# Where the seven-product couples stand in the ConvGLU of a two-layer encoder trunk, how many there are, and when the last gated tiles are raised

## The chip, the cores and the metric

The kernel runs on one core of a Trainium2 chip. A core has a matrix engine (TensorE, called PE in the profile, with PEld for its weight loads) and three elementwise engines: VectorE (DVE), ScalarE (ACT) and GpSimd (POOL). SyncE (SP) only issues DMA transfers here. Each engine takes its instructions in the order in which the program lists them, and they wait for one another by semaphores. SBUF is the on-chip memory; PSUM is where matmuls accumulate, in banks of 128 x 512 float32.

The metric is the device time of one execution in microseconds (us), lower is better. The kernel before takes 2427.54 us, the median of 3 runs (2427.39 to 2429.62).

## The reference

The input x has 256 tokens of width 2048. Two layers follow, each a pre-norm token mixer (layer 0 an mLSTM, layer 1 an HGRN2 recurrence) and a pre-norm ConvGLU. The change touches the ConvGLU alone:

```python
D_MODEL, SEQ, DEPTH, D_FF, CONV_W = 2048, 256, 2, 5504, 3

def conv_glu(hn, w_up, conv_w, conv_b, w_down):
    u = hn @ w_up                                  # (256, 2048) @ (2048, 11008)
    a, v = jnp.split(u, 2, axis=-1)
    ap = jnp.pad(a, ((0, 0), (1, 1), (0, 0)))
    c = conv_b
    for j in range(CONV_W):
        c = c + ap[:, j:j + 256] * conv_w[j]       # depthwise, along the tokens
    return (jax.nn.gelu(c, approximate=False) * v) @ w_down   # (256, 5504) @ (5504, 2048)

for layer in range(DEPTH):
    h = h + mixer(rmsnorm(h, norm_mix_g[layer]))
    h = h + conv_glu(rmsnorm(h, norm_ffn_g[layer]), ...)
out = rmsnorm(h, final_g)
```

## The kernel before

**Numbers.** All weights are float32 and are streamed once from HBM. For the matrix engine each operand is split into a high part, rounded to the reduced format fp32r, and a low part, what the rounding left. A product of two operands is three matmuls: high by high, high by low, low by high. For weights the high part `wh` is a cast on ACT (line 172 in the ConvGLU) and the low part `wl` a subtraction on DVE (line 173). There are four buffers of 1024 columns each for `wh` and for `wl`, and three of 2048 columns for the raw weights that a DMA fills; the split runs three pieces ahead of the matmuls.

**The ConvGLU.** The 43 tiles of 128 columns of D_FF are worked in three parts of 16, 16 and 11. A part first runs its up groups, of four tiles each (the last group of the part of 11 has three), and then a pair of down products, one for each half of the 2048 output columns. Groups and halves are objects of class `Pair`. A `Pair` walks its contraction in couples of two 128-row tiles: 8 couples for an up group (2048 rows) and for a down pair of a part of 16, and five couples and a half one ("H") for a down pair of the part of 11. A plan string names the form of each couple:

- "N" is the plain form. Two token halves by two column halves by two contraction tiles make 8 products, 24 matmuls of 512 columns.
- "S" is a Strassen-like form. It makes 7 products, 21 matmuls, from sums and differences of the operands. The weight differences are three DVE subtractions into the tile `T4` (lines 189, 191 and 192; of 1024, 512 and 512 columns). `T4` then goes through the same split as the raw weights: an S couple gives four pieces to split (of 1024, 512, 1024 and 1024 columns), an N couple two (of 1024). The differences of the x operand (`form`, split in its turn by lines 358 and 359) are made once per couple position and serve all `Pair`s that share x. N couples that stand before the last S of a plan need a small form too.
- Beside its four accumulators `c11` to `c22` (tiles `c1` and `c2`), a `Pair` with S couples needs three banks `m1`, `m6` and `m7`. It takes them at its first S. After its last S, `middle` adds them up into the SBUF tile `at` (`combine`, lines 1050 to 1054) and in a down pair adds `at` into the residual `hx` (line 1098). When all couples are through, `done` adds the accumulators (line 1083 in an up group, 1103 in a down pair).

**Raising.** A finished up group lies in `at` with tokens as rows. `raise_up` turns it tile by tile: four PE transposes per tile into a bank `pt` (line 1011), then ACT scale (1013), two DVE shifts of the convolution (1014 and 1015), ACT Gelu (1016), DVE product with v (1017), and the split into the gated tile `g` (1019 and 1020), plus the forms that the down plan wants. It is a side job: it makes a step whenever the matmul emitter's own clock (0.68 per product) has gone on by the value that the job yields. The banks `m1`, `m6`, `m7`, `pt` and all other small PSUM tiles come from one pool of four.

**What sets the order.** The code emits work in the order just told, and a scheduler that keeps a timeline of its own then places each engine's instructions. The order printed below is what it left. `UP_PLAN` and `DOWN_PLAN` in lines 23 and 24 are the two tables that the change edits.

Of the kernel before, what the change touches and what calls it, by code (L numbers as in the profile page):

```python
# [19 lines left out]
FT = 5504 // P  # L20
PARTS = ((0, 16), (16, 16), (32, 11))
GROUP = 4
UP_PLAN = "NNSNSNNN"
DOWN_PLAN = {16: "NNSNSNNN", 11: "NNNNNH"}
AH = 8
BH = 16
EPS = 1e-6
# [30 lines left out]
def trunk_kernel(ctx, tc, xT, x_d, fg_d, pp_d, cst_d, w_first, w_aq, w_ak, w_av, w_ao, w_aout,  # L58
# [59 lines left out]
    side = Side()  # L118
# [860 lines left out]
    def ffn(layer, norm, nxt):  # L979
# [17 lines left out]
        def raise_up(st):  # L997
            while not st["ready"]:
                yield 0.5
            at, w = st["at"], st["w"]  # L1000
            mp = box["mp"]
            for j in range(w // P):
                f, i = st["f"] + j, st["i"] + j
                if i % 2 == 0:
                    st["GT"].c2 = mp.tile([P, 2, T], F32, tag="c2", bufs=2, name="c2")
                c = st["GT"].c2[:, i % 2]
                pt = aux("pt")
                for n in range(2):
                    for t in range(2):
                        o = n * T + t * P  # L1010
                        pe.transpose(pt[:, o:o + P], at[:, t, n * 512 + j * P:n * 512 + (j + 1) * P], ident)  # L1011
                cw = [col("conv_w", (layer * 3 + k) * FT + f) for k in range(3)]
                act.activation(c, pt[:, 0:T], AF.Identity, scale=cw[1], bias=col("conv_b", layer * FT + f))
                dve.scalar_tensor_tensor(c[:, 1:T], pt[:, 0:T - 1], cw[0], c[:, 1:T], ALU.mult, ALU.add)
                dve.scalar_tensor_tensor(c[:, 0:T - 1], pt[:, 1:T], cw[2], c[:, 0:T - 1], ALU.mult, ALU.add)
                act.activation(c, c, AF.Gelu)
                dve.tensor_tensor(c, c, pt[:, T:2 * T], ALU.mult)
                g = slot(i, "g")
                act.copy(g[:, 0:T], c)
                dve.tensor_tensor(g[:, T:2 * T], c, g[:, 0:T].bitcast(F32), ALU.subtract)  # L1020
                st["GT"].x[i] = g
                if i % 2 and i // 2 in st["GT"].want:
                    st["GT"].forms[i // 2] = forms(st["GT"].c2, st["GT"].want[i // 2], mp, f"gf{i // 2}", mp)
                yield 2.5
            st["over"] = True

        class Gated:
# [29 lines left out]
        before = None  # L1057
        for part, (f0, nf) in enumerate(PARTS):
            GT = Gated(nf)
            for i in range(0, nf, GROUP):  # L1060
                w = min(GROUP, nf - i) * P
                st = dict(f=f0 + i, i=i, GT=GT, w=w, wait=[before] if before else [])
                before = st

                def middle(acc, st=st):
# [7 lines left out]
                def done(acc, st=st):  # L1073
                    w = st["w"]
                    plain = "at" not in st
                    if plain:
                        room(st)
                    for t in range(2):
                        d, v, sc = rows(acc["rows"][t], w), rows(st["at"][:, t], w), norm.rc[:, t:t + 1]
                        if plain:  # L1080
                            act.activation(v, d, AF.Copy, scale=sc)
                        else:
                            dve.scalar_tensor_tensor(v, d, sc, v, ALU.mult, ALU.add)
                    st["ready"] = True
                st["ready"] = False
                ch = Pair(w_up[layer, (f0 + i) // GROUP], UP_PLAN, norm.x, norm.form, lambda acc, done=done, st=st: (done(acc), side.push(raise_up(st))),
                          middle, w=w)
                ch.pool = lambda: box["mp"]
                chunks.append(ch)
            before = dict(wait=[before], over=True)  # L1090
# [43 lines left out]
    nf = FinalNorm()  # L1134
# [109 lines left out]
```

## Time and profile before

| what | value |
|---|---|
| median of 3 runs | 2427.54 us |
| the profiled execution | 2427.81 us, of which the span of its instructions is 2426.0 us |
| granted clock of the matrix engine, mean | 0.998 of full speed |
| ConvGLU of layer 0, first to last product of its `Pair`s | about 402 to 1115 us from the span's start |
| ConvGLU of layer 1, first product | 1704 us |

Times in the views are microseconds from the first instruction. In a row of instructions, `c<-wh,xt` reads "tile c written from tiles wh and xt", buffer numbers are left out (so `m` is any of m1, m6 and m7, and `T` is T4), `x16` is a count, and L207 is line 207 of the kernel. An engine's busy time says little when its work lies beside that of the engine that sets the pace, so the views that matter are those of one up group or one down pair.

Names for the stretches below: U0 to U3 are the four up groups of a part of 16 and D0 and D2 its two down pairs. The stretches quoted are of layer 0, part 1 (the second part), which runs from 666.8 to 929.4 us.

### The profile page before, as it was taken

What the parts mean: (1) busy time and instruction counts of PE and PEld (TensorE: products, weight loads), DVE (VectorE), ACT (ScalarE), POOL (GpSimd) and SP (SyncE); (2) the same over time, 40 slices, a digit from 0 to 9 for tenths busy, and PEclk for the clock granted to TensorE, in tenths of its full rate; (3) what the DMA queues carried; (4) which work ended last, traced back from release to release, by engine and by line L of the source; (5) the groups of instructions that cost most, each with busy time, mean ns of one, the idle gap of its engine ahead of it and who ended that gap; (6) DMA issues with size and microseconds to landing.
All of it is one profiled execution on the core that took longest, in us unless ns stands there. A gap on an engine that the chain in (4) does not pass through costs nothing.

```text
span 2426.0 us, 34357 instructions
## 1 busy us (share of the span) xinstructions
PE 2408.5 (99%) x13201; PEld 2012.4 (83%) x13201; DVE 1938.8 (80%) x2883; ACT 1364.1 (56%) x2024; POOL 165.1 (7%) x219
## 2 busy tenths in 40 slices
PE   9999999999999999999999999999999999999998
PEld 7888888888888888888888888888878888888886
DVE  7766667888889888866888889886798888987885
ACT  6655455656456555655555555555566555654654
POOL 0100000000000000001222222220000000000000
PEclk9999999999999999999999999999999999999999
DMA  7654555555655555465545544555555555556563
GB/s 288 199 182 157 191 174 174 197 185 186 207 179 199 185 195 205 163 210 170 171 172 174 173 166 168 173 174 178 187 181 201 191 196 189 175 204 208 177 208 137
DMA packets 65620, 451.73 MB, mean 186 GB/s; under 512 B 7584, under 2 KB 8096, under 8 KB 14000
## 3 DMA queue, kind: packets, MB, share of 16 engines
q1 hardware_dynamic: 63216, 442.91, 53.2%
q0 software_dynamic: 1232, 5.31, 0.9%
q8 instruction: 104, 1.70, 0.3%
q10 hardware_dynamic: 1008, 1.32, 0.2%
q14 instruction: 60, 0.49, 0.1%
HBM read 447.35 MB, written 2.16 MB: 185 GB/s over the span
## 4 chain that ended last, share of the span: by engine, by line
PE 97%; DVE 1%; ACT 1%; DMA 1%; issue 1%; SPq 0%; POOLq 0%; POOL 0%; ACTq 0%; DVEq 0%
PE c L207 49%; PE mm L330 10%; PE mm L321 7%; PE mm L320 7%; PE mm L322 7%; PE mm L337 5%; PE m L207 5%; PE pt L1011 2%; PE pn L676 1%; PE pd L863 1%; PE py L911 1%; PE pz L428 0%; PE pa L863 0%; DVE wl L173 0%; ACT wh L172 0%
## 5 line engine op out<-in xcount | busy, mean ns | idle before, releaser
L172 ACT CAST wh<-raw 128x1024 fp32r<-128x1024 f32 (+3 forms) x513 | 490.4, 987 | 323.4 <-PE c L207 303.1
L173 DVE TENSOR_TENSOR wl<-raw,wh 128x1024 fp32r<-128x1024 f32 (+3 forms) x513 | 576.0, 1144 | 115.3 <-ACT wh L172 113.8
L207 PE MATMUL c<-wh,xt 128*128 128x512 f32 (+1 forms) x2024 | 654.3, 389 | 0.9 <-ACT wh L172 0.4
L165 DVE TENSOR_TENSOR wl<-raw,wh 128x1024 fp32r<-128x1024 f32 (+1 forms) x340 | 414.2, 1222 | 196.4 <-ACT wh L164 195.6
L164 ACT CAST wh<-raw 128x1024 fp32r<-128x1024 f32 (+1 forms) x340 | 350.2, 1033 | 323.9 <-PE mm L322 163.8
L207 PEld LDWEIGHTS c<-wh,xt 128*128 128x128 f32 x2024 | 379.0, 188 | 73.1 <-ACT wh L172 3.3
L207 PE MATMUL c<-wl,xt 128*128 128x512 f32 (+1 forms) x1012 | 391.2, 388 | 0.4 <-DVE wl L173 0.4
L330 PE MATMUL mm<-xt,wh 128*128 128x512 f32 x1024 | 361.4, 396 | 0.9 <-DVE hx L1103 0.9
L207 PE MATMUL c<-wh,g 128*128 128x512 f32 x1000 | 323.7, 393 | 1.1 <-DVE hx L1103 0.9
L337 PE MATMUL mm<-xt,wl 128*128 128x256 f32 x1024 | 289.4, 283 | 0.0
L330 PEld LDWEIGHTS mm<-xt,wh 128*128 128x128 f32 x1024 | 192.1, 188 | 44.6 <-issue 1.3
L207 PE MATMUL c<-wh,F 128*128 128x512 f32 (+1 forms) x600 | 228.2, 390 | 0.0
L207 PEld LDWEIGHTS c<-wl,xt 128*128 128x128 f32 x1012 | 190.3, 188 | 40.4 <-DVE wl L173 6.2
L207 PEld LDWEIGHTS c<-wh,g 128*128 128x128 f32 x1000 | 187.7, 188 | 40.2 <-issue 2.1
L172 ACT CAST wh<-T 128x1024 fp32r<-128x1024 f32 (+1 forms) x120 | 124.7, 1039 | 141.8 <-PE c L207 139.2
L320 PE MATMUL mm<-wh,xt 128*128 128x512 f32 x512 | 202.1, 395 | 2.2 <-ACT xt L342 1.7
L321 PE MATMUL mm<-wl,xt 128*128 128x512 f32 x512 | 201.7, 394 | 0.6 <-DVE wl L165 0.6
L322 PE MATMUL mm<-wh,xt 128*128 128x512 f32 x512 | 200.7, 392 | 0.1
L207 PE MATMUL c<-wl,g 128*128 128x512 f32 x500 | 195.5, 391 | 0.0
L337 PEld LDWEIGHTS mm<-xt,wl 128*128 128x128 f32 x1024 | 193.3, 189 | 1.3
L173 DVE TENSOR_TENSOR wl<-T,wh 128x1024 fp32r<-128x1024 f32 (+1 forms) x120 | 144.8, 1207 | 59.8 <-ACT wh L172 58.5
L207 PEld LDWEIGHTS c<-wh,F 128*128 128x128 f32 x600 | 112.7, 188 | 23.5
(259 smaller groups left out, 3361.7 us busy)
## 6 DMA issues: line engine op xcount, KB each, us to landing
raw<-in_w_up SPq DMA_DIRECT2D x160, 1024.0 KB, 4.8
raw<-in_w_down SPq DMA_DIRECT2D x79, 1024.0 KB, 4.8
raw<-in_w_bq SPq DMA_DIRECT2D x48, 1024.0 KB, 5.0
raw<-in_w_ao SPq DMA_DIRECT2D x16, 1024.0 KB, 4.8
raw<-in_w_aout SPq DMA_DIRECT2D x16, 1024.0 KB, 4.8
raw<-in_w_bv SPq DMA_DIRECT2D x16, 1024.0 KB, 4.9
raw<-in_w_bg SPq DMA_DIRECT2D x16, 1024.0 KB, 4.8
raw<-in_w_bout SPq DMA_DIRECT2D x16, 1024.0 KB, 4.8
```

The source lines that it names most:

```text
L164: act.copy(wh[:, :m], r)
L165: dve.tensor_tensor(wl[:, :m], r, wh[:, :m].bitcast(F32), ALU.subtract)
L172: act.copy(wh[:, :m], r)
L173: dve.tensor_tensor(wl[:, :m], r, wh[:, :m].bitcast(F32), ALU.subtract)
L207: pe.matmul(acc[name][:, 0:w], a, b, start=name not in begun, stop=sp and i == 2)
L320: pe.matmul(ps[t], xh, wh[:, c], start=st, stop=False)
L321: pe.matmul(ps[t], xh, wl[:, c], start=False, stop=False)
L322: pe.matmul(ps[t], xl, wh[:, c], start=False, stop=sp)
L330: pe.matmul(ps[f], wh[:, c:c + P], x, start=st, stop=False)
L337: pe.matmul(ps[f][:, 0:T], wl[:, c:c + P], x[:, 0:T], start=False, stop=sp)
L676: pe.matmul(pn[:, 0:258], w, v, start=(i == 0), stop=(i == len(parts) - 1))
L1011: pe.transpose(pt[:, o:o + P], at[:, t, n * 512 + j * P:n * 512 + (j + 1) * P], ident)
```

## The change

Four tables and numbers change; no instruction of a new kind appears.

1. Up groups of a part, all but the last: `NNSNSNNN` becomes `SNSNSNNN`, three S couples in place of two.
2. The last up group of each part gets a plan of its own, `SNSNNNNN`: still two S couples, at the first and third place in place of the third and fifth.
3. Down pairs of 16: `NNSNSNNN` becomes `SNSNNNNN`, two S couples as before, at the first and third place.
4. Down pairs of 11: `NNNNNH` becomes `SNNNNH`, one S couple where there was none, and so `m1`, `m6`, `m7`, a `combine` and two additions into `hx` where there were none.
5. The raising of the last group of each part yields 0.8 in place of 2.5 after each tile, so its tiles follow each other sooner in the emitted order.

```diff
-UP_PLAN = "NNSNSNNN"
-DOWN_PLAN = {16: "NNSNSNNN", 11: "NNNNNH"}
+UP_PLAN = "SNSNSNNN"
+UP_LAST = "SNSNNNNN"
+PACE = 2.5
+PACE_LAST = 0.8
+DOWN_PLAN = {16: "SNSNNNNN", 11: "SNNNNH"}
...
-                yield 2.5
+                yield PACE_LAST if st['end'] else PACE
...
-                st = dict(f=f0 + i, i=i, GT=GT, w=w, wait=[before] if before else [])
+                st = dict(f=f0 + i, i=i, GT=GT, w=w, end=i + GROUP >= nf, wait=[before] if before else [])
...
-                ch = Pair(w_up[layer, (f0 + i) // GROUP], UP_PLAN, norm.x, norm.form, ...
+                ch = Pair(w_up[layer, (f0 + i) // GROUP], UP_LAST if i + GROUP >= nf else UP_PLAN, norm.x, norm.form, ...
```

After the change every line number that is named here is larger by 3 (207 is 210, 1083 is 1086).

Three places show how the instructions move. The first is DVE at the border between U0 and U1 (layer 0, part 1), where `done` of U0 (the two rows on `at<-c`) meets the first pieces of U1. Before, U1 begins with N couples, and T4 of its first S is made early:

```order
L173 TENSOR_TENSOR wl<-raw,wh 128x1024 x4
L189 TENSOR_TENSOR T_6040<-raw 128x1024
L1083 SCALAR_TENSOR_TENSOR at<-c_5726,rc,at 128x1024
L191 TENSOR_TENSOR T_6040<-raw,T_6040 128x512
L1083 SCALAR_TENSOR_TENSOR at<-c_5727,rc,at 128x1024
L192 TENSOR_TENSOR T_6040<-raw,T_6040 128x512
L173 TENSOR_TENSOR wl<-raw,wh 128x1024 x2
L1014 SCALAR_TENSOR_TENSOR c_6054<-pt,pp,c_6054 128x255
```

The same border on DVE after the change, from the last piece of U0 on:

```order
L176 TENSOR_TENSOR wl<-raw,wh 128x1024
L195 TENSOR_TENSOR T_6009<-raw,T_6009 128x512
L176 TENSOR_TENSOR wl<-raw,wh 128x512
L1086 SCALAR_TENSOR_TENSOR at<-c_5748,rc,at 128x1024
L1086 SCALAR_TENSOR_TENSOR at<-c_5749,rc,at 128x1024
L176 TENSOR_TENSOR wl<-T_6009,wh 128x1024 x2
L176 TENSOR_TENSOR wl<-raw,wh 128x1024 x2
L192 TENSOR_TENSOR T_6134<-raw 128x1024
L1017 SCALAR_TENSOR_TENSOR c_6075<-pt,pp,c_6075 128x255 x2
```

The two T4 pieces of U1's first S now stand behind `done` of U0 on DVE, and T4 of the second S and the first raised tiles follow at once.

The second place is DVE at the last S couple of U1 (its T4 is T_6202 before and T_6243 after), with the raising of U0's tiles between its pieces. Before:

```order
L191 TENSOR_TENSOR T_6202<-raw,T_6202 128x512
L173 TENSOR_TENSOR wl<-raw,wh 128x512
L357 TENSOR_TENSOR fe<-c_6114 128x256
L1020 TENSOR_TENSOR g_6154<-c_6114,g_6154 128x256
L173 TENSOR_TENSOR wl<-T_6202,wh 128x1024
L192 TENSOR_TENSOR T_6202<-raw,T_6202 128x512
L359 TENSOR_TENSOR F<-fe,F 128x256
L173 TENSOR_TENSOR wl<-T_6202,wh 128x1024
L173 TENSOR_TENSOR wl<-raw,wh 128x1024 x2
```

And on DVE after, at the third S couple of U1:

```order
L194 TENSOR_TENSOR T_6243<-raw,T_6243 128x512
L358 TENSOR_TENSOR fe<-c_6075,fe 128x128
L176 TENSOR_TENSOR wl<-T_6243,wh 128x1024
L1018 SCALAR_TENSOR_TENSOR c_6158<-pt,pp,c_6158 128x255
L195 TENSOR_TENSOR T_6243<-raw,T_6243 128x512
L362 TENSOR_TENSOR F<-fe,F 128x512
L1020 TENSOR_TENSOR c_6158<-c_6158,pt 128x256
L176 TENSOR_TENSOR wl<-T_6243,wh 128x1024
L176 TENSOR_TENSOR wl<-raw,wh 128x1024 x3
L1023 TENSOR_TENSOR g_6169<-c_6158,g_6169 128x256
```

Before, the fourth tile `g` is finished at this point; now only the third is, and the fourth is raised in the plain couples that follow.

The third place is PE in U1, where the products into `m6` (m_6169 before, m_6066 after; c_6032 and c_6033 before, and c_6063 and c_6064 after, are the accumulators c1 and c2) stand against the transposes. Before, at the first S couple:

```order
L207 MATMUL c_6033<-wl,F 128x512
L207 MATMUL c_6033<-wh,F 128x512
L207 MATMUL m_6170<-wl,F 128x512
L207 MATMUL m_6170<-wh,F 128x512
L207 MATMUL m_6169<-wh,F 128x512
L207 MATMUL c_6033<-wh,xt_3287 128x512
```

And on PE after, at the second S couple, where the first product into `m6` of the first S couple has been put off to:

```order
L210 MATMUL m_6066<-wh,F 128x512
L210 MATMUL m_6066<-wl,F 128x512
L210 MATMUL m_6066<-wh,F 128x512 x2
L210 MATMUL c_6064<-wl,F 128x512
L210 MATMUL c_6064<-wh,F 128x512
L210 MATMUL m_6067<-wl,F 128x512
L210 MATMUL m_6067<-wh,F 128x512
L210 MATMUL c_6064<-wh,xt_3290 128x512
L1014 MATMUL pt<-cst,at 128x128 x4
```

The bank that `m6` takes holds a `pt` until then, and with three of the four banks in use for `m1`, `m6` and `m7` the later tiles are transposed one at a time through the fourth.

More of the change, by code (lines that the diff above doesn't have):

```diff
@@ L1085, in ffn @@
                 st["ready"] = False
-                ch = Pair(w_up[layer, (f0 + i) // GROUP], UP_PLAN, norm.x, norm.form, lambda acc, done=done, st=st: (done(acc), side.push(raise_up(st))),
+                ch = Pair(w_up[layer, (f0 + i) // GROUP], UP_LAST if i + GROUP >= nf else UP_PLAN, norm.x, norm.form, lambda acc, done=done, st=st: (done(acc), side.push(raise_up(st))),
                           middle, w=w)
```

## The prediction

> **What bounds the kernel now.** I read the page first: busy times and the chain that ended last.
>
> ```profile
> span 2426.0 us, 34357 instructions
> PE 2408.5 (99%) x13201; PEld 2012.4 (83%) x13201; DVE 1938.8 (80%) x2883; ACT 1364.1 (56%) x2024; POOL 165.1 (7%) x219
> PE 97%; DVE 1%; ACT 1%; DMA 1%; issue 1%; SPq 0%; POOLq 0%; POOL 0%; ACTq 0%; DVEq 0%
> ```
>
> PE makes 97% of the chain, so a matmul taken away is time saved, unless what feeds PE is late. Whether it is late is a question of each stretch, so next comes the view by stretches, each from the first product of a `Pair` to that of the next, in layer 0, part 1: U0 to U3, D0, D2, then U1 and U2 of the part of 11 and its first down pair.
>
> ```profile
> core 0: us, PE busy (x) PEld busy (x) DVE busy (x) ACT busy (x) POOL busy (x), PEclk, DMA share, GB/s
> 666.80:709.00 42.20, 42.20 (x188) 34.95 (x187) 33.12 (x33) 22.56 (x25) 0.00 (x0) 1.00 0.58 200
> 709.00:753.40 44.40, 44.40 (x203) 36.18 (x202) 38.81 (x52) 27.54 (x39) 0.00 (x0) 1.00 0.56 189
> 753.40:798.00 44.60, 44.60 (x203) 36.28 (x202) 38.70 (x54) 27.68 (x39) 0.00 (x0) 1.00 0.55 188
> 798.00:842.90 44.90, 44.82 (x204) 36.25 (x203) 39.99 (x54) 27.40 (x38) 0.00 (x0) 1.00 0.55 189
> 842.90:887.20 44.30, 44.30 (x203) 36.25 (x202) 39.01 (x49) 24.80 (x35) 0.00 (x0) 1.00 0.56 190
> 887.20:929.40 42.20, 42.20 (x188) 34.91 (x187) 33.94 (x34) 20.61 (x23) 0.00 (x0) 1.00 0.58 201
> 971.60:1016.00 44.40, 44.40 (x204) 36.10 (x202) 37.74 (x49) 26.50 (x37) 0.00 (x0) 1.00 0.50 167
> 1016.00:1050.60 34.60, 34.40 (x203) 33.78 (x203) 29.78 (x44) 22.28 (x37) 0.00 (x0) 1.00 0.59 199
> 1050.60:1083.10 32.50, 31.61 (x146) 25.81 (x145) 22.89 (x37) 17.84 (x24) 0.00 (x0) 1.00 0.60 208
> ```
>
> U0 and D2 have 186 products and nothing else on PE: 42.2 us. Stretches with raising have 16 transposes more and take 44.3 where PE never waits (D0), so a transpose costs 2.1 / 16 = 0.13. U1 waits about 0.1, U2 0.3, U3 0.6. DVE has 5.6 us to spare in U1, but 9.1 in U0. That spare is what the change spends.
>
> How far DVE is ahead is seen in the rows themselves. DVE at the end of U1's second S couple:
>
> ```profile
> 732.85 0.70 DVE L192 TENSOR_TENSOR T<-raw,T 128x512 f32<-128x512 f32 x1
> 733.45 0.43 DVE L359 TENSOR_TENSOR F<-fe,F 128x256 fp32r<-128x256 f32 x1
> 734.72 1.23 DVE L173 TENSOR_TENSOR wl<-T,wh 128x1024 fp32r<-128x1024 f32 x1 [0.84 <-ACT wh L172]
> 735.86 2.35 DVE L173 TENSOR_TENSOR wl<-raw,wh 128x1024 fp32r<-128x1024 f32 x2
> ```
>
> and PEld just there:
>
> ```profile
> 737.13 0.19 PEld L207 LDWEIGHTS c<-wl,xt 128*128 128x128 f32 x1 [0.37 <-DVE wl L173]
> ```
>
> The first piece of the last row ends near 735.86 + 1.22 = 737.08, and the weight load that reads it starts at 737.13: the lead of DVE over PE is already used up once per group, at its last S couple. In the plain couples it comes back, up to what four buffers hold. The wait there is the T4 chain: last subtraction ended (733.55), cast on ACT, next piece at 734.72, which is 1.17 us.
>
> **The change, part by part.**
>
> *Fewer matmuls.* Every S in place of an N saves 3 matmuls. Eight up groups of each layer (3 + 3 + 2) get a third S, 16 in all; pairs of the part of 11 get one each, two in layer 0 and one in layer 1 (its other half is no `Pair`). 19 x 3 = 57, all of 512 columns, since the three-tile group keeps two S. The price of one is PE's start-to-start:
>
> ```profile
> 929.17 0.39 PE L207 MATMUL c<-wh,g 128*128 128x512 f32 x1
> 929.39 0.39 PE L207 MATMUL c<-wh,xt 128*128 128x512 f32 x1
> ```
>
> about 0.22, and over D2 42.2 / 186 = 0.2267. So 57 x 0.2267 = **12.9 us less** on PE.
>
> *More work on DVE.* The groups of U1:
>
> ```profile
> L173 DVE TENSOR_TENSOR wl<-raw,wh 128x1024 fp32r<-128x1024 f32 x14 | 16.9, 1223 | 3.0 <-ACT wh L172 3.0
> L173 DVE TENSOR_TENSOR wl<-T,wh 128x1024 fp32r<-128x1024 f32 x4 | 4.9, 1224 | 1.3 <-ACT wh L172 1.3
> L1083 DVE SCALAR_TENSOR_TENSOR at<-c,rc,at 128x1024 f32<-128x1024 f32 x2 | 2.6, 1284 | 0.3 <-PE c L207 0.2
> L189 DVE TENSOR_TENSOR T<-raw 128x1024 f32<-128x1024 f32 x2 | 2.4, 1222 | 0.0
> L191 DVE TENSOR_TENSOR T<-raw,T 128x512 f32<-128x512 f32 x3 | 2.1, 686 | 0.0
> L1014 DVE SCALAR_TENSOR_TENSOR c<-pt,pp,c 128x255 f32<-128x255 f32 x4 | 1.9, 481 | 0.9 <-ACT c L1013 0.9
> ...
> L1020 DVE TENSOR_TENSOR g<-c,g 128x256 fp32r<-128x256 f32 x4 | 1.7, 422 | 0.0
> ...
> L173 DVE TENSOR_TENSOR wl<-raw,wh 128x512 fp32r<-128x512 f32 x2 | 1.4, 693 | 0.0
> ```
>
> The next instruction starts before the one ahead has ended:
>
> ```profile
> 751.79 1.28 DVE L1083 SCALAR_TENSOR_TENSOR at<-c,rc,at 128x1024 f32<-128x1024 f32 x1
> 752.99 0.68 DVE L191 TENSOR_TENSOR T<-raw,T 128x512 f32<-128x512 f32 x1
> 753.61 1.28 DVE L1083 SCALAR_TENSOR_TENSOR at<-c,rc,at 128x1024 f32<-128x1024 f32 x1
> 754.81 0.68 DVE L192 TENSOR_TENSOR T<-raw,T 128x512 f32<-128x512 f32 x1
> 755.41 2.35 DVE L173 TENSOR_TENSOR wl<-raw,wh 128x1024 fp32r<-128x1024 f32 x2
> ```
>
> so 512 columns cost 0.60 (754.81 to 755.41) and 1024 cost 2.35 - 1.22 = 1.13. An S adds 1.13 + 2 x 0.60 of subtractions and turns two pieces of 1024 into three and one of 512, 1.13 + 0.60 more: **4.1 us of DVE per S**. The form at position 0 is now the large one, +0.7 in U1 (four operations of 128 and one of 512 for two of 256, scaled from the same rows); U2 and U3 lose forms at places 3 and 4. Hence U1: 38.8 + 4.1 + 0.7 = 43.6 of DVE against 44.4 - 0.7 = 43.7 of PE, U2 about 42.2 of 43.9. In U0 37.2 of 41.5: covered.
>
> *Whether U1 holds.* From the order, between the second `done` row of U0 and the last T4 piece of the third S, DVE has 14 instructions of 1024 columns, 7 of 512, 5 of 256, 4 of 128, 6 shifts and the `done` row: 14 x 1.13 + 7 x 0.60 + 5 x 0.33 + 4 x 0.20 + 6 x 0.40 + 1.20 = 26.1 (256 and 128 scaled by 1.13 - 0.60 per 512 columns; a shift 481 - 422 = 59 ns over a 256). PE has, from U0's last matmul to the one that reads that piece, 109 matmuls and 16 transposes: 24.7 + 2.1 = 26.8. DVE starts `done` after that last matmul:
>
> ```profile
> 753.17 0.63 PE L207 MATMUL c<-wh,xt 128*128 128x512 f32 x2
> ```
>
> against 753.61 above: 0.44 later. The T4 chain adds 1.87 (1.17 and the subtraction's 0.70) where the order gives it 0.60 + 0.60 + 0.33: 0.3. DVE is through at 0.44 + 26.1 + 0.3 + 0.1 = 26.9 against 26.8, and the piece behind is needed 4 matmuls (0.9) later for 1.13 of work: PE waits 0.3. Waits of DVE for ACT in the same place before were the 0.84 above, mostly this chain; a few tenths more are likely. Bounds: 0 (no gaps, the lead carried over from the plain couples) and 2.5 (the idle of DVE ahead of the T4 pieces, the shifts and `done` in U1 before: 1.3 + 0.9 + 0.3 in the groups above; the 3.0 ahead of the plain pieces is mostly full buffers). I take a wait of 0.6 for U1 and U2, nearest to the sum, 0.4 more than now. Ten groups have three S and raising: **+4.0**.
>
> *Last groups and 16-wide down pairs* (U3, D0, D2) keep their S count; the S couples come first, behind `done`. U3's DVE loses a form (1.4): -0.1 each, **-0.4** for four. In D0 the tiles of U3 are raised in the same stretch as the S couples; the faster pace moves them nearer, but three of the four banks are held, so they still go one at a time. The last tile must be there for the last couple, 40 us into D0, and in the order it stands about 5 us ahead. I take +0.2 for each D0 (0 to 1): **+0.8**. D2 and U0 have no raising: 0.
>
> *Pairs of 11.* DVE gets an S (4.1), a `combine` (1.13 + 2 x 0.60) and two additions of 1.13: 22.9 + 8.7 = 31.6 against 31.8 of PE, with raising ending in mid-pair. Before, this pair waited 0.9 (32.50 against 31.61 busy), and the new work lies behind the plain couples' slack: 0, bounds -0.7 and +1 each.
>
> *First group of each layer* begins with an S whose form comes straight from the norm, and holds three banks while the last x tiles are transposed: 0 to 1, I take 0.2, **+0.4** for both.
>
> *ACT and DMA.* An S adds a cast of 1024 and one of 512 to ACT, some 1.5 us on 27.5 of 44. Bytes are the same; T4 needs its raw tile whole, and waited for DMA twice in layer 0:
>
> ```profile
>   DMA raw<-in_w_up: 2.1, 2
> ```
>
> with DMA at 0.55 to 0.60 in the stretches, I take 0. SP issues the same transfers, POOL is untouched.
>
> Sum: -12.9 + 4.0 - 0.4 + 0.8 + 0.4 = -8.1. The profiled execution took 2427.8, of which 2426.0 is the span; its time stands 0.3 above the median. 2427.8 - 8.1 = 2419.7, against the median 2419.4; I say **2419.5 us**.
>
> [...] By the rows above DVE overlaps: 1.28 long, the next 1.20 later. [...]
>
> **The rivals.**
>
> *The cover holds everywhere.* DVE goes ahead in the plain tails, the ten groups wait as little as U1 and U2 now: 2427.5 - 12.9 to -14 = 2413.5 to 2415. For it: the sum is a tie. Against: the lead was already at 0.05 us in U1 with two S.
>
> *DVE gaps take most of it.* Each of the ten groups waits 1 to 1.8 instead of 0.2: -12.9 + 10 x 0.8 to 1.6 + 0.8 = -4 to +4, 2423 to 2431.
>
> *Slower: the raise chain blocks PE.* PE's fourth set of transposes in U1 waits for the one free bank, released by the product row L1020 (1017 before), and stands in PE's queue before the last `m6` products; by the sums above that release comes only 0.2 us ahead of PE's place. If DVE keeps the 2.5 us of idle that it had there, every one goes straight to PE: ten groups x 2.3 = 23, less 12.9: about +10, 2437. It decides from 1.3 us of gaps per group on. Against it: much of that idle was DVE standing at full buffers.
>
> *Slower: DVE cannot overlap.* If each DVE instruction cost its whole length, U1 would need the sum of its durations, some 43 by its groups, plus 1.22 + 2 x 0.69 + 1.22 + 0.69 = 4.5: 47.6 and so 3.2 more than now in ten groups, +32 less 9 x 0.7 elsewhere: 2453. The overlap in the rows speaks against it. [...]
>
> **How the numbers follow.** A measurement here tells 0.2% (4.9 us) from no change. My forecast, 2416 to 2422.7: 0.48. Cover holds: 0.17. Gaps take most: 0.20, nearly all of it within 0.2%. Blocked raise chain: 0.11. No overlap: 0.02; elsewhere slower: 0.02. So faster 0.65, same 0.20, slower 0.15. The range 2414 to 2429 leaves out the two slower cases and the edges of the others, about 0.2; the likeliest case alone spans 2416 to 2422.7.
>
> **What would show it.** PE matmuls 57 fewer. U0 and D2 at 41.5 and 42.2 without waits. U1 and U2 near 44.2, with PEld waiting for `wl` at the third S; DVE above 42 busy there. D0 near 44.5. The forecast is wrong if U1 takes over 45 (gaps), if PE waits before `pt` or the first `m6` (banks), or if the part of 11's pairs grow by over a microsecond.

## The result and the profile after

The changed kernel takes 2418.45 us, the median of 5 runs (2417.42 to 2418.99), against 2429.61 us (2427.39 to 2430.08) of the kernel before on the same chip: a ratio of 0.9956, 95% interval 0.9942 to 0.9971. The forecast was 2419.5 us. The profiled execution has a span of 2416.7 us, 9.3 us less than before. The sum is close, its terms are not: U3, put at -0.4 us, and D2 with the later U0, put at 0, turned out at -3.2 and +3.0.

The lines of the page that answer to those shown of before (span, busy times, engine shares of the chain):

```profile
span 2416.7 us, 34392 instructions
PE 2396.5 (99%) x13144; PEld 2001.0 (83%) x13144; DVE 2015.4 (83%) x2993; ACT 1393.4 (58%) x2062; POOL 166.0 (7%) x219
PE 90%; DVE 7%; issue 1%; ACT 1%; DMA 1%; SPq 0%; POOLq 0%; POOL 0%; ACTq 0%; DVEq 0%
```

There are 57 matmuls fewer (13201 to 13144), and DVE now stands in 7% of the chain instead of 1%: PE waits more often for what DVE makes. The same nine stretches as in the prediction (U0 to U3, D0, D2 of layer 0, part 1, then U1, U2 and the first down pair of the part of 11):

```profile
core 0: us, PE busy (x) PEld busy (x) DVE busy (x) ACT busy (x) POOL busy (x), PEclk, DMA share, GB/s
665.60:707.40 41.80, 41.80 (x184) 34.15 (x183) 35.58 (x36) 23.87 (x27) 0.00 (x0) 1.00 0.58 201
707.40:751.70 44.30, 44.21 (x201) 35.68 (x201) 43.41 (x59) 29.02 (x41) 0.00 (x0) 1.00 0.52 173
751.70:796.10 44.40, 44.12 (x201) 35.65 (x200) 42.68 (x57) 28.85 (x40) 0.00 (x0) 1.00 0.56 193
796.10:840.10 44.00, 44.00 (x203) 36.45 (x202) 37.45 (x47) 27.27 (x37) 0.00 (x0) 1.00 0.56 194
840.10:884.20 44.10, 44.10 (x204) 36.46 (x203) 39.56 (x49) 25.04 (x35) 0.00 (x0) 1.00 0.53 185
884.20:926.80 42.60, 42.60 (x187) 34.70 (x186) 33.90 (x33) 20.60 (x23) 0.00 (x0) 1.00 0.62 216
968.60:1012.80 44.20, 44.11 (x200) 35.64 (x199) 41.74 (x57) 28.11 (x40) 0.00 (x0) 1.00 0.51 170
1012.80:1047.40 34.60, 34.60 (x203) 33.75 (x202) 31.27 (x47) 22.79 (x37) 0.00 (x0) 1.00 0.57 188
1047.40:1078.10 30.70, 30.70 (x143) 25.39 (x142) 28.22 (x36) 18.14 (x25) 0.00 (x0) 1.00 0.55 186
```

U1 and U2 lost three matmuls each, 0.68 us, but only 0.2 us of their length. U3, which lost none, is 0.8 us shorter; D2 is 0.4 us longer; the pair of 11 is 1.8 us shorter. Where PE now stands, read from the weight loads (PEld) of part 1, in U0, U1 and D2 (the bracket holds the wait before the row and what ended it):

```profile
668.27 0.19 PEld L210 LDWEIGHTS c<-wh,xt 128*128 128x128 f32 x1 [0.21 <-ACT wh L175]
691.17 0.19 PEld L210 LDWEIGHTS c<-wl,xt 128*128 128x128 f32 x1 [0.33 <-DVE wl L176]
...
732.92 0.42 PEld L1014 LDWEIGHTS pt<-cst,at 128*128 128x128 f32 x4 [0.49 <-PE m L210]
734.01 0.19 PEld L210 LDWEIGHTS c<-wh,xt 128*128 128x128 f32 x1 [0.40 <-ACT wh L175]
735.46 0.19 PEld L210 LDWEIGHTS c<-wl,xt 128*128 128x128 f32 x1 [0.38 <-DVE wl L176]
...
886.93 0.19 PEld L210 LDWEIGHTS c<-wh,g 128*128 128x128 f32 x1 [0.29 <-ACT wh L175]
899.67 0.19 PEld L210 LDWEIGHTS c<-wl,g 128*128 128x128 f32 x1 [0.33 <-DVE wl L176]
```

U1's waits for weights are at its third S couple, as forecast, and make 0.40 + 0.38. Just ahead of them the transposes of the fourth raised tile wait too (the row at 732.92). That row names PE's own product, but DVE's product L1020, the last reader of the one free bank, ended within 0.1 us of it:

```profile
732.39 0.41 DVE L1020 TENSOR_TENSOR c<-c,pt 128x256 f32<-128x256 f32 x1
```

In all ten raising groups with three S these transposes start 0.15 us after L1020 has ended, and 0.25 to 0.52 us behind PE's pace, 3.8 us in all. So PE does wait before `pt`, which the prediction named as a sign of the bank rival. It costs little by itself, because the weights wanted next come later still: in run 2 below U1 of part 1 has no such wait and is only 0.14 us shorter.

But U0 and D2, where nothing is raised and DVE has 6 and 9 us to spare, wait as well: at the opening couple and at the last one, 0.21 + 0.33 and 0.29 + 0.33. An S couple takes 1.13 + 2 x 0.60 of differences and 3 x 1.13 + 0.60 of pieces, 6.3 us of DVE, for 21 x 0.2267 = 4.8 us of PE. A group that opens with one has no plain couple ahead in which a lead could be built. Nor is DVE short at the opening: T4 of D2's first couple was ready at 878.1 us, and ACT then stood idle for 4.31 us, until PE's last products of D0 gave a buffer free for its cast:

```profile
883.93 2.00 ACT L175 CAST wh<-T 128x1024 fp32r<-128x1024 f32 x2 [4.31 <-PE c L210]
```

The four buffers bound the lead there.

The change of each kind of stretch, from first product to the next stretch's first product, both layers, against the terms of the prediction:

| stretches | us, before to after | products alone | rest | the prediction's rest |
|---|---|---|---|---|
| ten raising groups with three S | -1.2 | -6.8 | +5.6 | +4.0 |
| U0, first of a layer (2) | -1.3 | -1.4 | 0 | +0.4 |
| U0, others (4) | -1.4 | -2.7 | +1.3 | 0 |
| U3 (4) | -3.2 | 0 | -3.2 | -0.4 |
| D0 (4) | -0.7 | 0 | -0.7 | +0.8 |
| D2 (4) | +1.7 | 0 | +1.7 | 0 |
| last groups of 11 (2) | -0.4 | 0 | -0.4 | 0 |
| pairs of 11 (3), with all outside the ConvGLU | -2.7 | -2.0 | -0.7 | 0 |
| all | -9.3 | -12.9 | +3.6 | +4.8 |

Two single waits of this execution, 0.8 us in U2 of layer 1 and 0.6 in the first D0, hardly recur in the later profiles; without them the ten groups' rest is +4.8 and D0's -1.3. What lies outside the ConvGLU took 0.5 us more than before; up to the next product behind each, the three pairs alone took 3.2 us less, a rest of -1.2.

### The profile page after: what moved, and what is told of

It is laid out like the page before. It is cut to its first block, busy times and chain, and to the rows that moved or that the text cites. A ratio compares the mean times of both kernels' runs of the same rounds, so it can differ in the third digit from the quotient of the medians.

```text
span 2416.7 us, 34392 instructions
## 1 busy us (share of the span) xinstructions
PE 2396.5 (99%) x13144; PEld 2001.0 (83%) x13144; DVE 2015.4 (83%) x2993; ACT 1393.4 (58%) x2062; POOL 166.0 (7%) x219
## 4 chain that ended last, share of the span: by engine, by line
PE 90%; DVE 7%; issue 1%; ACT 1%; DMA 1%; SPq 0%; POOLq 0%; POOL 0%; ACTq 0%; DVEq 0%
PE c L210 42%; PE mm L333 10%; PE mm L323 7%; PE mm L324 7%; PE mm L325 7%; PE m L210 5%; PE mm L340 5%; DVE wl L176 3%; PE pt L1014 1%; PE pn L679 1%; PE pd L866 1%; DVE T L192 1%; PE py L914 1%; PE pz L431 0%; PE pa L866 0%
## 5 line engine op out<-in xcount | busy, mean ns | idle before, releaser
L210 PE MATMUL c<-wh,xt 128*128 128x512 f32 (+1 forms) x1944 | 620.1, 386 | 0.0
L176 DVE TENSOR_TENSOR wl<-raw,wh 128x1024 fp32r<-128x1024 f32 (+3 forms) x513 | 566.3, 1120 | 53.7 <-ACT wh L175 53.3
L210 PEld LDWEIGHTS c<-wh,xt 128*128 128x128 f32 x1944 | 363.8, 188 | 71.4 <-ACT wh L175 4.8
L210 PE MATMUL c<-wl,xt 128*128 128x512 f32 (+1 forms) x972 | 375.0, 386 | 0.0
L175 ACT CAST wh<-T 128x1024 fp32r<-128x1024 f32 (+1 forms) x158 | 161.2, 1039 | 185.9 <-PE c L210 155.3
L210 PEld LDWEIGHTS c<-wl,xt 128*128 128x128 f32 x972 | 182.4, 188 | 39.2 <-DVE wl L176 5.1
L176 DVE TENSOR_TENSOR wl<-T,wh 128x1024 fp32r<-128x1024 f32 (+1 forms) x158 | 188.0, 1206 | 31.1 <-ACT wh L175 22.8
L210 PE MATMUL c<-wl,g 128*128 128x512 f32 x514 | 200.9, 391 | 0.3 <-DVE wl L176 0.3
L210 PE MATMUL c<-wh,F 128*128 128x512 f32 (+1 forms) x500 | 196.0, 395 | 0.8 <-ACT wh L175 0.8
L210 PE MATMUL m<-wh,F 128*128 128x512 f32 (+1 forms) x316 | 117.0, 396 | 0.0
```

The lines of the kernel that those rows point to most:

```text
L175: act.copy(wh[:, :m], r)
L176: dve.tensor_tensor(wl[:, :m], r, wh[:, :m].bitcast(F32), ALU.subtract)
L210: pe.matmul(acc[name][:, 0:w], a, b, start=name not in begun, stop=sp and i == 2)
```

## The experiments

Each was timed in 5 rounds beside the kernel before on the same chip, so ratios compare. Beside each stands what it is to be set against: the change itself at 0.9956 (0.9942 to 0.9971).

**1. The places without the extra couples.**

```diff
-UP_PLAN = "SNSNSNNN"
+UP_PLAN = "SNSNNNNN"
-DOWN_PLAN = {16: "SNSNNNNN", 11: "SNNNNH"}
+DOWN_PLAN = {16: "SNSNNNNN", 11: "NNNNNH"}
```

> The new positions without the added couples: every up group S N S N N N N N, the down pairs of 16 as in the change, the pairs of 11 without a couple; as many products as before the change. Theory (raising groups with three couples are held by DVE's work, those with two by PE): the two raising groups of a part then run as the last groups do in the changed kernel, 44.05 us, 0.4 to 0.55 below the kernel before, ten of them -4.5; last groups -3.2, first down pairs -1.3, second down pairs +1.7, all as in the changed kernel: -7.3 together, 2422.3 us (2420.5 to 2424). Then the added couples are worth only some 4 us of their 12.9. Rival (the positions give nothing, the missing products give all): 2428.5 to 2430.5.

Measured: 2421.41 us, ratio 0.9972 (0.9961 to 0.9984), a span 6.4 us below the one before. The theory's number is nearly met and the rival's is not. Its stretches in part 1, U0 to D2:

```profile
664.80:707.30 42.50, 42.50 (x187) 34.72 (x186) 31.78 (x31) 22.58 (x25) 0.00 (x0) 1.00 0.54 198
707.30:751.40 44.10, 44.10 (x203) 36.46 (x202) 39.60 (x54) 27.41 (x39) 0.00 (x0) 1.00 0.52 186
751.40:795.50 44.10, 44.10 (x203) 36.46 (x202) 38.78 (x52) 27.36 (x38) 0.00 (x0) 1.00 0.53 191
795.50:839.60 44.10, 44.10 (x203) 36.46 (x202) 37.45 (x47) 27.28 (x37) 0.00 (x0) 1.00 0.52 186
...
883.70:926.30 42.60, 42.60 (x187) 34.67 (x186) 33.90 (x33) 20.59 (x23) 0.00 (x0) 1.00 0.59 213
```

The three raising groups are all alike, 44.1 us, with no wait of PEld: the 0.4, 0.5 and 0.8 us that U1, U2 and U3 had above that before were waits that go when the couples stand first and third. U0 grows by 0.3 us and D2 by 0.4. The run also keeps the faster pace of the change, which run 7 prices at 3.2 us, all of it in D0 and D2. So places and pace together take 6.4 us off the span with the very same products, and the 57 matmuls, worth 12.9 us on PE, bring 2.9 us more (2419.6 to 2416.7). DVE's work in U1 is 39.6 us here and 38.8 before: the waits went although DVE has more to do.

**2. The old places in the down pairs of 16.**

```diff
-DOWN_PLAN = {16: "SNSNNNNN", 11: "SNNNNH"}
+DOWN_PLAN = {16: "NNSNSNNN", 11: "SNNNNH"}
```

> The changed kernel with the couples of the 16-tile down pairs back at the third and fifth place. Theory: second down pairs lose their wait at the first weights (42.6 to 42.2 us), but an N and an S form more are made per part while the up groups raise, and DVE has no slack in the third group (42.7 of 44.4 us): +0.6 there, +0.2 in the last group, +0.3 in the first down pair, -0.4 in the second, times four: +2.8, 2421.2 us (2419.5 to 2423). Rival (the 0.4 us of the second down pairs is all that the place costs): 2416.7 us.

Measured: 2415.4 us, ratio 0.9949 (0.9937 to 0.9962). The rival is right: by the stretches this part of the change costs about 0.4 us in each D2 and brings nothing elsewhere, though the two intervals overlap. U2 and D2 of part 1:

```profile
750.70:795.10 44.40, 44.16 (x200) 35.64 (x199) 43.35 (x59) 29.14 (x41) 0.00 (x0) 1.00 0.52 189
...
883.20:925.40 42.20, 42.20 (x188) 34.93 (x187) 35.25 (x36) 19.91 (x23) 0.00 (x0) 1.00 0.54 195
```

D2 is back at 42.2 us, and PEld has no wait in it. U2 carries 0.7 us more of DVE, 43.35 instead of 42.68, and is as long as it was: its length isn't set by DVE's total. That is where the theory failed.

**3. More DVE work in each couple.**

```diff
             dve.tensor_tensor(T4[:, 3 * w:4 * w], raw[:, 3 * w:4 * w], T4[:, 2 * w:3 * w], ALU.subtract)
+            dve.tensor_tensor(T4[:, 3 * w:4 * w], raw[:, 3 * w:4 * w], T4[:, 2 * w:3 * w], ALU.subtract)
```

> The changed kernel with the last subtraction of each couple's weights made twice (0.68 us of DVE more per couple, the value the same; nothing changes on PE, in PSUM or in the transfers). Theory (DVE's work sets the raising groups with three couples): these have 43.4 of 44.25 us of DVE, so 2.05 more is 1.2 to 2.05 us longer, ten of them +12 to +20; groups that raise nothing (35.6 of 41.8), last groups and down pairs 0 to 0.2 each: 2431 to 2440 us, middle 2435. Rival (the PSUM bank chain or PE's own pace sets them, DVE is cover): all groups of one kind move alike, by 0 to 0.2 each: 2418.5 to 2422 us.

Measured: 2468.54 us, ratio 1.0165 (1.0151 to 1.0178), 50 us above the changed kernel. Both numbers were missed. U1, D0 and D2 of part 1 (the line numbers behind the added one are larger by 1):

```profile
718.90:766.40 47.50, 45.12 (x201) 35.56 (x200) 45.47 (x62) 28.86 (x41) 0.00 (x0) 1.00 0.47 168
...
859.10:904.40 45.30, 45.09 (x203) 36.08 (x203) 40.83 (x51) 24.89 (x35) 0.00 (x0) 1.00 0.53 194
904.40:947.30 42.90, 42.90 (x188) 34.69 (x188) 35.20 (x35) 20.79 (x23) 0.00 (x0) 1.00 0.55 199
```

The ten raising groups grow by 33 us, U3 by 1.1 each, D0 by 1.1 each, D2 by 0.25. A U1 grows by 3.2 us for 2.05 us of work, and DVE is idle for 2 us of it: 0.8 for ACT's cast of a T4 piece, 1.3 ahead of `done`, where it has nothing left but to wait for PE's last products. PEld shows where PE stands, at the third couple:

```profile
746.80 0.19 PEld L211 LDWEIGHTS m<-wh,F 128*128 128x128 f32 x1 [1.25 <-ACT wh L175]
748.06 0.19 PEld L211 LDWEIGHTS m<-wl,F 128*128 128x128 f32 x1 [0.96 <-DVE wl L176]
750.10 0.19 PEld L211 LDWEIGHTS c<-wl,xt 128*128 128x128 f32 x1 [1.06 <-DVE wl L176]
```

1.25 + 0.96 + 1.06 = 3.3 us, where the changed kernel has 0.8; another 1.2 stands at the couple before. In the plain couples behind it DVE gets ahead again, but a delay of PE is not won back. Taken with run 2, this is what sets a raising group: the DVE work that stands ahead of the last couple's weights, not the group's total. Why it is 3.3 and not 2.05 isn't settled: with one more instruction in its timeline, the scheduler also put form operations of the raised tiles ahead of weight pieces in this place, and that part was not measured by itself.

**4. The same subtraction on POOL.**

```diff
-            dve.tensor_tensor(T4[:, 3 * w:4 * w], raw[:, 3 * w:4 * w], T4[:, 2 * w:3 * w], ALU.subtract)
+            pool.tensor_tensor(T4[:, 3 * w:4 * w], raw[:, 3 * w:4 * w], T4[:, 2 * w:3 * w], ALU.subtract)
```

> The changed kernel with the last subtraction of each couple's weights on POOL instead of DVE (0.68 us of DVE less per couple; POOL's nearest row is 1.31 us for 128x256, so some 2 us each here, one per couple). Theory (DVE's work): the raising groups with three couples lose most of the 0.55 us that they stand above their products (43.65 us), ten times -0.35: -3.5, 2415 us (2413.5 to 2417). Rival (PSUM banks): no change, 2418 to 2419. Rival (POOL's result comes late or slows DVE): over 2420 us, with PE's weight loads waiting for the last weights of the couple in every group.

Measured: 2425.61 us, ratio 0.9989 (0.998 to 0.9998), 7 us above the changed kernel. The third reading, that POOL slows DVE, is the one that held, though not in every group: U3 and the down pairs keep their length within 0.1 us. Groups of this run (count, then busy time and mean ns of one):

```profile
L195 POOL TENSOR_TENSOR T<-raw,T 128x512 f32<-128x512 f32 x75 | 154.1, 2055 | 1256.1 <-DVE T L194 1094.9 <-DVE fe L356 131.7 <-ACT xt L345 29.5
...
L176 DVE TENSOR_TENSOR wl<-raw,wh 128x512 fp32r<-128x512 f32 x75 | 67.6, 902 | 15.0 <-ACT wh L175 14.5
```

and the second of them in the changed kernel:

```profile
L176 DVE TENSOR_TENSOR wl<-raw,wh 128x512 fp32r<-128x512 f32 x75 | 51.3, 684 | 9.0 <-ACT wh L175 8.6
```

One pair of such rows on the timeline of the run, POOL and DVE:

```profile
720.24 1.29 POOL L195 TENSOR_TENSOR T<-raw,T 128x512 f32<-128x512 f32 x1 [13.99 <-DVE T L194]
...
720.81 1.27 DVE L176 TENSOR_TENSOR wl<-raw,wh 128x512 fp32r<-128x512 f32 x1
```

POOL's row ends at 721.53, and the DVE row that began beside it ends 0.55 us later, at 722.08: it took 1.27 us where the row at 731.27 in this run, with no POOL row beside it, took 0.68. POOL's rows differ too: the one at 732.69, which began 0.02 us behind a DVE row of 1.22 us (`wl<-T,wh`, 128x1024), took 2.35 us, the one at 720.24 took 1.29. In both pairs the row that began later is the long one; what held it is not shown. Not every row is stretched: two DVE rows of L1018, which read PSUM, took 0.87 us together while POOL's row at 720.24 began, at the usual 0.48 each. DVE's busy time in U1 is 43.56 us, where the changed kernel has 43.41, though three subtractions less are in it.

**5. The raised tiles of the other groups later.**

```diff
-PACE = 2.5
+PACE = 5.0
```

> The changed kernel with 5.0 instead of 2.5 between the raised tiles of a group that is not a part's last: the same work on every engine, later in the group. Theory, as it stands after the first four runs (not DVE's total but DVE's work before the third couple's last weights sets a raising group; after them the weights are up to 3.8 us early): raising work that moves behind the third couple shortens the wait of 0.55 us there by 0.1 to 0.4, ten times: 2416 us (2414 to 2418). Rival (DVE's total per group): no change, 2418 to 2419. Rival (the one free PSUM bank): a later start of the raising has it end later, so the group's third couple waits for the sums' tile: over 2420 us.

Measured: 2463.4 us, ratio 1.0143 (1.0127 to 1.0159). U1 and U2 of part 1:

```profile
717.80:761.30 43.50, 43.50 (x201) 35.87 (x201) 40.88 (x54) 26.62 (x37) 0.00 (x0) 1.00 0.53 193
761.30:810.40 49.10, 45.27 (x201) 36.98 (x200) 44.47 (x61) 30.03 (x41) 0.00 (x0) 0.97 0.47 173
```

U1 does what the theory said, more than it said: 43.45 us and no wait. That is the length of a raising group with three S when nothing is late; the changed kernel's U1 stands 0.8 above it. But U2 grows by 4.7 us and U3 by 5.0, and nearly the whole loss has one cause, in the waits of PEld over the span (total, times, longest):

```profile
PEld pt L1014 <- DVE at L1086: 42.5, 12, 4.3
```

The fourth tile is now transposed behind U1's third couple. There is one row tile `at`, so U1's sums can't go into it before that; they are finished late, and the transposes of U1's own tiles, which stand early in U2 on PE's queue, wait for them. The third theory came nearest: it has the time over 2420 us and names the sums' tile, but puts the wait at the group's third couple and down to the PSUM bank. Run 9 tests the row tile.

**6. The third couple one place later.**

```diff
-UP_PLAN = "SNSNSNNN"
+UP_PLAN = "SNSNNSNN"
```

> The changed kernel with the third couple of the up groups at the sixth place instead of the fifth (S N S N N S N N; the same products, one N form more per layer). Theory (work before the third couple's last weights): one couple of ordinary tiles more, 5.4 us of PE for 2.3 us of DVE, stands ahead of the third couple, so the wait of 0.55 us there goes nearly wholly: 43.75 us per raising group, ten times -0.45, 2414.2 us (2413 to 2416). Rival (DVE's total): no change, 2418 to 2419.5. Rival (PSUM banks): three of four banks are held 5.4 us longer, the transposes of the raised tiles wait longer on the fourth: 2420 to 2425 us.

Measured: 2415.25 us, ratio 0.9945 (0.9932 to 0.9958), inside the theory's range. U1, U2 and U3 of part 1:

```profile
707.20:750.60 43.40, 43.40 (x201) 35.90 (x200) 41.87 (x57) 27.91 (x38) 0.00 (x0) 1.00 0.53 189
750.60:794.70 44.10, 43.92 (x200) 35.66 (x199) 42.91 (x59) 28.88 (x41) 0.00 (x0) 1.00 0.53 191
794.70:839.00 44.30, 44.30 (x203) 36.30 (x202) 38.35 (x49) 27.81 (x39) 0.00 (x0) 1.00 0.55 200
```

U1 loses its whole wait, the banks held 5.4 us longer notwithstanding, so the bank rival falls. U2 has 0.3 us less, not 0.45, and U3 0.3 more: with later sums DVE's work slides into the next group (U3 has 38.35 us of it instead of 37.45). Some 0.15 us each is lost in the later U0, 0.4 in the first ones, and 0.75 in the last groups of 11.

**7. The old pace in the groups raised beside the down pairs.**

```diff
-PACE_LAST = 0.8
+PACE_LAST = 2.5
```

> The changed kernel with the old pace, 2.5 for 0.8, in the groups whose raising runs beside the first down pair: undoes that part of the change alone. Theory: the first down pairs have 39.6 of 44.05 us of DVE and are PE's, the pace only moves when the last tiles are there, and these are needed late: +0.1 each, six times: 2419 us (2418 to 2420). Rival (the sooner raising is what took the 0.8 us from the last groups or the 0.3 us from the first down pairs): 2420 to 2423 us.

Measured: 2421.17 us, ratio 0.997 (0.9958 to 0.9982). The rival's range. D0 and D2 of part 1, and the waits of PEld there:

```profile
840.50:884.80 44.30, 44.30 (x203) 36.37 (x202) 39.09 (x49) 24.66 (x34) 0.00 (x0) 1.00 0.51 184
884.80:927.90 43.10, 42.76 (x187) 34.60 (x186) 34.45 (x34) 20.86 (x23) 0.00 (x0) 1.00 0.58 212
```

```profile
882.19 0.30 PEld L210 LDWEIGHTS c<-wh,g 128*128 128x128 f32 x2 [0.38 <-DVE g L1023]
888.08 0.19 PEld L210 LDWEIGHTS c<-wh,g 128*128 128x128 f32 x1 [0.76 <-ACT wh L175]
```

With the old pace D0 waits for its last gated tile (0.38 for `g`), and D2 waits 0.76 instead of 0.29 for `wh` in its opening couple: 0.3 us in D0 and 0.5 in D2, 3.2 us over four parts. DVE is not what holds D2, since that tile was finished at 882.14; ACT's cast of D2's first T4 piece gets its buffer from PE 0.25 us after D2's first product, where the changed kernel has it 0.26 us before. So the pace halves what D2 loses by opening with a couple.

D0 is as long here as in the kernel before, 44.3 us, but not for the same reason. In the kernel before it waits for weights, 18 us into the stretch:

```profile
861.24 0.19 PEld L207 LDWEIGHTS c<-wl,g 128*128 128x128 f32 x1 [0.25 <-DVE wl L173]
```

There it has no wait for `g`. With the faster pace D0 has neither wait, at the new places (run 1 and, but for one single wait, the change) or at the old (run 2). So D0's gain needs the pace.

**8. Three couples in every up group, other places below.**

```diff
-UP_PLAN = "SNSNSNNN"
-UP_LAST = "SNSNNNNN"
+UP_PLAN = "SNSNNSNN"
+UP_LAST = "SNSNNSNN"
-DOWN_PLAN = {16: "SNSNNNNN", 11: "SNNNNH"}
+DOWN_PLAN = {16: "NSNSNNNN", 11: "SNNNNH"}
```

> A version meant to beat both kernels: all up groups S N S N N S N N (a third couple in the last groups of a part too), 16-tile down pairs N S N S N N N N, the rest as in the change. Theory: -4.5 as in the run with the third couple at the sixth place; the last groups lose 0.68 us of products and gain 0.1 of waits, the four of 512 columns -2.3, the two of 384 -0.8; the second down pairs no longer start with a couple, -0.4 each, -1.7: 2409 us (2407 to 2413). Rival (banks or DVE's total): the last groups have 37.5 + 4.1 us of DVE in 43.4, so they would gain too, but the others not: 2414 to 2416.

Measured: 2438.62 us, ratio 1.0043 (1.003 to 1.0056): wrong by 30 us. The last groups got longer (U3 by 0.7 each) with 42.9 us of DVE, and the down pairs in which their tiles are raised too: D0 of 16 by 2.1 us each, the first pair of 11 by 5.3 and 6.5 us. In layer 0 that pair has a wait of 3.96 us for the sums in `at`, as in run 5; its own plan is the change's, and run 6 has the same places in the other groups without this loss. D0 of part 1 waits 0.29 + 0.90 + 1.09 us for weights at its first couple. A group whose tiles are needed in the very next stretch is, by this run, the wrong one for a third couple. Which part the down pairs' new places have in D0's 2.1 us stays open.

**9 and 10. A second row tile, with the later pace and without.** One of two buffers of a norm's row factors makes the room in both; run 9 has `PACE = 5.0` as well, run 10 keeps 2.5.

```diff
-            st["at"] = box["mp"].tile([P, 2, 1024], F32, tag="at", bufs=1, name="at")
+            st["at"] = box["mp"].tile([P, 2, 1024], F32, tag="at", bufs=2, name="at")
...
-            self.R_ = ev.tile([P, T], F32, tag="R", bufs=2, name="R")
+            self.R_ = ev.tile([P, T], F32, tag="R", bufs=1, name="R")
```

> The run with pace 5.0 again, with two buffers for the row tile that is raised (at) instead of one, and one of two buffers of a norm's row factors given up for room. Theory (with pace 5.0 the fourth tile is transposed behind the third couple, the next group's sums can't go to the one row tile before that, and its own transposes, on PE's queue, wait for them: 3.8 us at the start of the third group): with a second row tile that wait goes, the third and the last groups lose their 5 us and keep what the second groups showed, 43.45 us instead of 44.3: 2410.5 us (2408 to 2414). Rival (the late work itself, DVE 44.5 us in the third group, is what costs): 2450 to 2464 us. Rival (two-thirds of it is PSUM banks): 2425 to 2445.

> The changed kernel with two buffers for the row tile (at) and the pace left at 2.5 (one of two buffers of a norm's row factors given up for room): the last run without its pace of 5.0. Theory (the later raising is what shortens the second groups from 44.25 to 43.85 us; the second row tile only lifts the limit on how late it may be): second and third groups as in the changed kernel, 44.25 and 44.4 us, the two groups of 384 columns somewhat shorter: 2418 us (2416.5 to 2419.5). Rival (the second row tile itself, which lets the sums be combined before the raising has ended, gives it): 2413 to 2415.5 us.

Measured: 2414.38 us, ratio 0.9945 (0.9931 to 0.996), with the later pace; 2420.24 us, ratio 0.9967 (0.9955 to 0.9979), without. The wait that cost 42.5 us in run 5 is, in run 9:

```profile
PEld pt L1014 <- DVE at L1086: 1.8, 4, 0.5
```

So the single row tile was the cause of run 5's loss. U1 in run 9 is 43.85 us and in run 10 44.2, as in the changed kernel: the later raising shortens U1, and the second row tile by itself does nothing there. It has a price: in both runs D0 waits 0.4 us for ACT's copy `v` of its sums and is 0.3 us longer. U2 keeps 44.3 us in both, so run 9 ended 4 us above the number set for it, and run 10 2 us above its own; both lie just outside their ranges.

**11. Runs 2 and 6 together.** `UP_PLAN` as in run 6, `DOWN_PLAN` as in run 2, and the row factors' buffer as above for room.

> Third couple of the up groups at the sixth place together with the old places (third and fifth) in the down pairs of 16, everything else as in the change; one of two buffers of a norm's row factors is given up for room. Theory (the two edits are independent: the one took some 2 us beside the changed kernel in its call, the other some 2 us, half of that by second down pairs 0.42 us shorter): 2413.5 us (2412 to 2415.5). Rival (the two more forms of the down pairs now do cost, since DVE's work in the third group is what the later couple relieved): 2415.5 to 2418.

Measured: 2415.25 us, ratio 0.9951 (0.9938 to 0.9964). By its time it lies at the upper end of the theory's range and just below the rival's, so the time does not decide. The stretches do, for the rival: the two don't add. D2 has its 42.2 us, but U3, with the forms that the old places want and the work that the later couple sends it, is 44.85 us instead of 44.05.

**12. A second couple in the pairs of 11.**

```diff
-DOWN_PLAN = {16: "SNSNNNNN", 11: "SNNNNH"}
+DOWN_PLAN = {16: "SNSNNNNN", 11: "SNSNNH"}
```

> The changed kernel with a second couple in the pairs of 11 (S N S N N H instead of S N N N N H): three couples in all, nine products less. Theory (the pairs of 11 are PE's, DVE has 26.6 to 28.2 of 30.7 us there and 4.1 more fits just in the second layer and not in the first, whose sums of the next norm come in that time): -0.68 in two pairs, 0 to +2 in the first pair of layer 0: 2417.5 us (2416 to 2420). Rival (the first couple took 1.8 us in layer 0, of it 1.1 a wait of the pair behind it that no second couple can take again): the same number at best, never below 2416.4.

Measured: 2422.04 us, ratio 0.9977 (0.9968 to 0.9986), above the theory's range; the rival's bound, never below 2416.4, holds. The first pair has 30.2 us of DVE in 30.3 and gains 0.4 us of its 0.7; the second one of layer 0 is 1.8 us longer, and the mixer behind it 2.4. Of the two numbers tried, one couple is the better.

Versions 2, 6, 9 and 11 lie at 0.9945 to 0.9951, below the change's 0.9956, but every interval overlaps its interval: none is shown to be faster than it.

## Why the prediction was right, and where it was not

**The products, -12.9 us: right.** 57 matmuls fewer, and the two first groups of a layer, which wait for nothing, lost 1.33 us where six matmuls make 1.36.

**The ten raising groups, +4.0: right in kind and place, measured +5.6.** The wait is at the third couple, for `wh` and `wl`. Two sizes were off, against each other: the length without a wait is 43.45 us (runs 5 and 6), not 43.7, and the wait 0.8 to 1.0, not 0.6. The waits before were larger too, by run 1 0.4 us in U1 and 0.5 in U2 where the prediction read 0.1 and 0.3, so that a group lost about 0.5 us and not 0.4. The reason was only half right. The prediction weighed DVE's work up to the third couple's last piece, which run 3 confirms as the place, but held U1's total of 43.6 against 43.7 as well, and run 2 shows that 0.7 us more of the total doesn't matter.

**U3, -0.4: this term failed, it measured -3.2.** The prediction named U3's wait of 0.6 us and then costed the move of its couples by DVE's total alone (one form less). Run 1 shows what it left out: with the couples first and third the wait goes wholly, there and in U1 and U2. It is the places and not the pace: run 7, with the old pace, has the same 44.05 us in U3.

**D2 and the later U0, 0: failed, +1.7 and +1.3.** "No raising" was taken for "no wait". A stretch that opens with a couple waits at it, where the buffers come free too late, and at its last one, whatever DVE has to spare in all; run 2 takes the wait away by putting two plain couples first, run 1 shows the U0 part by itself.

**D0, +0.8: wrong in sign, -0.7.** The 44.3 us that was called a length without waits had a wait of 0.3 for weights in it. With the faster pace no wait is left, at the old places or the new; with the old pace and the new places a wait for the last gated tile, which the prediction feared, takes its place (run 7). The price of a transpose, 0.13, was read off the same length; without the wait it is 0.12.

**First groups of a layer, +0.4: 0.** No wait showed there.

**Pairs of 11, 0 (-0.7 to +1 each): -1.2 by themselves, -0.7 with what lies outside.** The first pair of layer 0 gave 1.8 us for three matmuls, a rest of -1.1, beyond its bound; the other two came out near 0. The 1.1 is a wait that the kernel before and run 1 have at the border to the next pair, here in the kernel before:

```profile
1083.09 0.19 PEld L207 LDWEIGHTS c<-wh,g 128*128 128x128 f32 x1 [1.30 <-issue]
```

With a couple in the pair it is gone. Why is not shown: the profile names nothing that it waits for.

**The rivals.** "The cover holds everywhere" gave too low a time, but its neglected half, waits that the new places remove, is why the sum came out. The raise chain over the one free bank is there, as that rival said: PE waits before the fourth set of transposes in all ten groups, for L1020, but 0.25 to 0.52 us and not 2.3, and the weights behind are later still. Run 6 holds the banks longer and is no slower. DVE does overlap: its rows of 1.22 us in D0 start 1.13 to 1.14 us apart (874.81, 875.95, 877.08), and U1, which that rival put at 47.6 us, takes 44.3.

The forecast's time was met because 5.8 us of gains that it missed (U3 2.8, D0 1.5, pairs of 11 0.7, last groups of 11 0.4, first groups 0.4) stood against 4.6 us of waits that it missed or made too small (ten groups 1.6, D2 1.7, U0 1.3). That these nearly cancel is luck.

## What to carry to other kernels

When one engine prepares what another consumes through a few buffers, compare their work from the start of the stretch up to each piece, not over the stretch: a stretch with 6 us to spare can still wait in its first five. Place the heavy steps where a lead has been built up, move side work behind the last of them, and then look for the buffer that this order holds (here the one row tile). Before taking a stretch as free of waits, go through its rows for a single short one. And when a stretch is as long as before, see whether it still waits for the same thing.

## What the runs showed of the hardware

POOL's subtraction of 128x512 took 2.06 us on average, three times DVE's 0.68 (the rows in U1 of part 1 from 1.29 to 2.49), and the DVE row `wl<-raw,wh` of 512 columns that began beside one of them ended 0.55 us after it (run 4; over the span such rows took 902 ns on average instead of 684): moving one of three subtractions off DVE made DVE no freer in U1, 43.56 us busy instead of 43.41.

A long wait of PE cost more than itself in run 5. Five-microsecond stretches around the wait at the start of U2 show the granted clock in the column after POOL's:

```profile
760.00:765.00 5.00, 2.12 (x10) 1.42 (x8) 4.97 (x8) 4.40 (x6) 0.00 (x0) 1.00 0.30 121
765.00:770.00 5.00, 4.05 (x12) 3.22 (x13) 5.00 (x7) 2.69 (x4) 0.00 (x0) 0.66 0.00 0
770.00:775.00 5.00, 5.00 (x25) 4.12 (x24) 4.96 (x8) 2.55 (x4) 0.00 (x0) 1.00 0.34 102
```

and the weight loads behind the wait come at about half the rate of those ahead of it, 0.43 us apart (766.80 to 767.23) instead of 0.23 (761.28 to 761.51):

```profile
765.95 0.14 PEld L1014 LDWEIGHTS pt<-cst,at 128*128 128x128 f32 x1 [4.25 <-DVE at L1086]
...
766.80 0.33 PEld L210 LDWEIGHTS c<-wh,xt 128*128 128x128 f32 x1
767.23 0.33 PEld L210 LDWEIGHTS c<-wl,xt 128*128 128x128 f32 x1
```

U2 is 5.7 us longer than the 43.45 us of a group without waits. PE's first start behind the wait is 4.0 us behind its pace: it waits 3.8 us behind a product of 0.39, and its pace is 0.23. The other 1.7 is put down to the matmuls that follow at the lowered clock: by estimate from the steps above, nine of that stretch's 12 at 0.43 us instead of 0.23 make 1.8. In run 3, whose longest wait in U1 is 1.25 us, the clock of that stretch stays at 1.00.
